# A hybrid decoder block on one Trainium2 core: the split left operands of the output projection placed at 16 different byte offsets

## The chip, the core and the metric

The kernel runs on one core of a Trainium2 chip. The core has TensorE (matmuls, "PE", and the loads of its stationary operand, "PEld"), VectorE ("DVE"), ScalarE ("ACT"), GpSimd ("POOL"), and SyncE ("SP"), which here only issues DMAs. SBUF is the on-chip memory of 128 partitions from which the engines read their operands; PSUM takes TensorE's results. The metric is the device time of one execution in microseconds (us), as the median of several runs.

## What is computed

One decoder block on a sequence of 2048 positions and 1024 channels, in float32. The reference, cut to the stages that matter here:

```python
h = rms_norm(x, g_norm[l]) * (1.0 + scale[:, None, :]) + shift[:, None, :]
proj = h @ w_in[l]
...
y_rnn = (hr * jax.nn.silu(z_rnn.astype(jnp.float32))).astype(dt) @ w_out_rnn[l]
...
y_attn = (o * jax.nn.silu(z_attn.astype(jnp.float32))).astype(dt) @ w_out_attn[l]
merged = jax.nn.sigmoid(g_r + bg_r) * y_rnn + jax.nn.sigmoid(g_a + bg_a) * y_attn
x = x + gate[:, None, :] * (merged @ w_o[l])
return rms_norm(x, g_final)
```

The change lies in the last product, `merged @ w_o`, which the kernel calls the output projection.

## The kernel before

Each product of two float32 matrices is made of three matmuls in the type `float32r`: both operands are split into a high part (a rounded copy, written by ScalarE in `hi_act`, L157) and a low part (what the copy leaves out, written by VectorE in `lo_dve`, L166, or by GpSimd in `lo_pool`, L163). `mm3` (L151) then adds high x high, high x low and low x high into one PSUM tile. `mm` (L149) is the only place that issues matmuls, so all of them carry that line; the profile tells them apart by their tiles. In `mm` the operand called `l` (lhsT) is the stationary one that is loaded by a weight load, and `r` is the moving one that streams past it.

The program has four stages. First the normalised input and the input projection (PSUM tiles X, Z, W, V, Y; operands S, T and b12), with the recurrence of the RG-LRU branch (tiles xr, xc, pg, gh and gl) between its products. Then the attention (sc, pT, o, with operands kq, pp, vh and wh), with the branch output projections (pj) filled in between. `steps` (L1652) is the generator of these fillers: eight jobs, two branches by four column blocks of 512 positions, each of eight row tiles m and eight steps k; each step issues one `mm3`. What the two branches give is multiplied by its gates, added, and stored to `meT` in HBM. Last, the output projection.

The output projection is `output(n)` (L1833), called for n = 0 to 3. Each call yields four row blocks r of 128 positions, 16 in all, and after each row block eight steps of `steps` are drawn, as long as there are any (L1864 to 1867). For each row block:

- xo, 128 x 1024, is loaded from x, and mraw, 128 x 8 x 128, from `meT` (L1837 and L1840).
- mh, the high part of mraw, is written by ScalarE, and ml, the low part, by VectorE (L1843 and L1844). Both tiles have 4096 bytes in a partition and three buffers each, which the row blocks use in turn.
- For each half q of the 1024 output columns a PSUM tile pq (four buffers) gets 8 x 3 = 24 matmuls. The stationary operand is a 128 x 128 piece of mh or ml, the moving one 512 columns of oh or ol, the split of w_o times the gate, which `output_operands` (L1825) makes once. A row block so has 48 weight loads and 48 matmuls.
- VectorE adds pq to xo (L1851), ScalarE squares and sums (L1854), small steps make the factor of the norm (L170 to L179), VectorE applies it (L1856), and SP stores ob (L1857).

The order of the attention stage is written out by hand; that of this last stage is made by a scheduler when the program is built, from the order in which the code issues the instructions. Each engine runs its own instructions in the program's order and waits on semaphores for the others. SBUF addresses are given by pools. The pool `fp` holds, in this order, oh, ol, gf, gate_b, xo, mraw, mh, ml, ob and ss, and the pool `wr` behind it holds pieces of the branch weights. Both lie in memory that the attention's pool `ap` has left.

Of the kernel before, what the change touches and what calls it, by code (L numbers as in the profile page):

```python
# [11 lines left out]
F32R = mybir.dt.float32r  # L12
# [8 lines left out]
P = 128  # L21
S = 2048
D = 1024
KT = D // P
# [65 lines left out]
def decoder_block(ctx, tc, x, c, positions, g_norm, w_mod, b_mod, w_in, b_gate, conv_w, conv_b,  # L90
# [4 lines left out]
    def T(pool, shape, dt, tag, **kw):  # L95
        cnt[0] += 1
        return pool.tile(shape, dt, tag=tag, name=f"{tag}_{cnt[0]}", **kw)
# [53 lines left out]
    def mm3(o, lh, ll, rh, rl, first=True, last=True, **kw):  # L151
        mm(o, lh, rh, first, False, **kw)
        mm(o, lh, rl, False, False, **kw)
        mm(o, ll, rh, False, last, **kw)

    def hi_act(o, i):
        nc.scalar.activation(o, i, AF.Copy)  # L157
# [7 lines left out]
    def lo_dve(o, i, h):  # L165
        return nc.vector.tensor_tensor(o, i, h.bitcast(F32), ALU.subtract).ins  # L166
# [14 lines left out]
    def rstd(ss):  # L181
        rstd_first(ss)
        rstd_last(ss)
# [921 lines left out]
    for t in range(6):  # L1105
        pieces = []
        i0 = t * P
        while i0 < (t + 1) * P:
            hd, i = divmod(i0, 96)
            n = min(96 - i, (t + 1) * P - i0)  # L1110
# [154 lines left out]
    for f in range(2):  # L1265
# [20 lines left out]
        n = 0  # L1286
# [528 lines left out]
    fp = pools.open("fp", bufs=1)  # L1815
# [17 lines left out]
    def output(n):  # L1833

        for r in range(4):
            xo = T(fp, [P, D], F32, "xo", bufs=2)
            nc.sync.dma_start(xo[:], xv[n, r])  # L1837
            t = T(fp, [P, KT, P], F32, "mraw", bufs=2)
            c0 = n * CH + r * P
            nc.sync.dma_start(t[:], meT[:, c0 : c0 + P].rearrange("(k p) j -> p k j", p=P))  # L1840
            th = T(fp, [P, KT, P], F32R, "mh", bufs=3)
            tl = T(fp, [P, KT, P], F32R, "ml", bufs=3)
            hi_act(th[:], t[:])  # L1843
            lo_dve(tl[:], t[:], th[:])  # L1844
            for q in range(2):
                cq = slice(q * CH, (q + 1) * CH)
                ps = T(pq, [P, CH], F32, "pq")
                for k in range(KT):
                    mm3(ps[:], th[:, k, :], tl[:, k, :], oh[:, k, cq], ol[:, k, cq],
                        first=k == 0, last=k == KT - 1)  # L1850
                nc.vector.tensor_tensor(xo[:, cq], ps[:], xo[:, cq], ALU.add)  # L1851
            ob = T(fp, [P, D], F32, "ob", bufs=1)
            ss = T(fp, [P, 3, 1], F32, "ss", bufs=4)
            nc.scalar.activation(ob[:], xo[:], AF.Square, accum_out=ss[:, 0])  # L1854
            rstd(ss)
            nc.vector.scalar_tensor_tensor(ob[:], xo[:], ss[:, 1], gf[:], ALU.mult, ALU.mult)  # L1856
            nc.sync.dma_start(outv[n, r], ob[:])  # L1857
            yield
# [5 lines left out]
    for n in range(NB):  # L1864
        for _ in output(n):
            for _ in range(KT):
                next(fill, None)
# [30 lines left out]
```

## Time and profile before

| what | value |
|---|---|
| median of 3 runs | 2237.18 us (2236.78 to 2237.21) |
| the profiled execution, its own time | 2235.07 us |
| span of its instructions | 2233.3 us |
| TensorE clock granted, mean | 0.994 |
| first and last matmul of the output projection start at | 1981.5 and 2224.6 us |
| weight loads and matmuls of the output projection | 768 each |

How to read the profile: it shows one execution. Busy times are in us, the mean of one instruction in nanoseconds (ns). A group such as `pq<-oh,mh` names the tile that is written and the tiles that are read. Matmuls are pipelined: the length shown for one of them (389 ns for 512 columns) overlaps the next one's, so their pace is read from the distance of their starts. The chain of waits is followed back from the last instruction: at each step to what released it, or to the instruction before it on its engine. In a list of stretches or of the timeline "x" is the number of instructions; "idle before" an instruction is time in which its engine had nothing to do.

### The profile page before, as it was taken

Reading aid. Unit: us, or ns where it says so; the run is one execution under the profiler, and the core shown is the slowest. Engines: PE = TensorE matmul, PEld = TensorE weight load, DVE = VectorE, ACT = ScalarE, POOL = GpSimd, SP = SyncE. Lnnn points to the kernel's source line nnn. Section 1 sums busy time; section 2 is a strip of 40 time slices with the busy share of each in tenths; the row PEclk is TensorE's granted clock in tenths of the full one; section 3 lists DMA queues with packets and bytes.
Section 4 is the critical chain, followed back from the end, with each engine's and each line's share of the span. In section 5 each row is a group of like instructions: output and inputs, shape, how many; then the busy total and the mean of one; then the engine's idle time right before and its main releaser. Section 6 shows DMA issues by size and latency. Waiting matters only on the chain.

```text
span 2233.3 us, 33998 instructions
## 1 busy us (share of the span) xinstructions
PE 2185.9 (98%) x11422; PEld 1851.1 (83%) x11422; DVE 1348.6 (60%) x2380; ACT 1256.2 (56%) x2481; POOL 978.3 (44%) x734
## 2 busy tenths in 40 slices
PE   8999999999999999999999999999999998999998
PEld 5998888888778998888888887888888887878886
DVE  5838887878455815544545442566677777666443
ACT  6638678668543627556556202667778887533211
POOL 2457777767557422222222102455566665332100
PEclk9999999999999999999999999999999999999999
DMA  8367887887998378888888988988988887899542
GB/s 286 117 211 259 287 295 269 292 282 269 326 282 288 114 229 271 286 286 280 287 288 278 343 291 286 285 265 259 271 255 264 246 262 216 254 338 284 155 132 85
DMA packets 428626, 573.64 MB, mean 257 GB/s; under 512 B 72134, under 2 KB 292514, under 8 KB 427428
## 3 DMA queue, kind: packets, MB, share of 16 engines
q1 hardware_dynamic: 390612, 451.73, 64.9%
q10 hardware_dynamic: 37648, 119.70, 14.0%
q8 instruction: 90, 1.47, 0.3%
q14 instruction: 84, 0.69, 0.1%
q0 software_dynamic: 192, 0.05, 0.0%
HBM read 357.44 MB, written 213.91 MB: 256 GB/s over the span
## 4 chain that ended last, share of the span: by engine, by line
PE 55%; DMA 6%; DVE 3%; ACT 3%; issue 2%; POOL 2%; SPq 1%; ACTq 0%; POOLq 0%; DVEq 0%
PE pj L149 11%; PE X L149 8%; PE V L149 7%; PE pq L149 7%; PE sc L149 4%; PE W L149 4%; PE Z L149 4%; PE o L149 4%; PE Y L149 3%; PE pT L1501 1%; DMA R<-in_w_in_dram 1%; PE pg L149 1%; PE pT L1514 1%; POOL S L163 1%; DMA gaT<-ev 1%
## 5 line engine op out<-in xcount | busy, mean ns | idle before, releaser
L149 PE MATMUL pj<-yh,S 128*128 128x512 f32 x1024 | 367.8, 403 | 9.7 <-ACT yh L157 4.8
L163 POOL TENSOR_TENSOR S<-R,S 128x512 fp32r<-128x512 f32 x168 | 252.2, 1509 | 175.0 <-ACT S L157 64.9
L149 PE MATMUL V<-T,S 128*128 128x512 f32 x1344 | 324.6, 390 | 3.7 <-DVE t L450 3.5
L149 PE MATMUL X<-T,S 128*128 128x512 f32 x1344 | 324.5, 390 | 2.9 <-POOL S L163 1.9
L149 PEld LDWEIGHTS V<-T,S 128*128 128x128 f32 x1344 | 251.8, 188 | 58.4 <-DVE t L450 2.4
L149 PEld LDWEIGHTS X<-T,S 128*128 128x128 f32 x1344 | 251.4, 188 | 58.0 <-POOL S L163 2.8
L149 PEld LDWEIGHTS pj<-yh,S 128*128 128x128 f32 x1024 | 193.2, 189 | 47.8 <-ACT yh L157 6.7
L149 PE MATMUL pj<-yl,S 128*128 128x512 f32 x512 | 201.6, 394 | 6.2 <-POOL yl L163 5.1
L1417 ACT ACTIVATE pp<-pp,st 128x256 f32<-128x256 f32 (+3 forms) x256 | 133.8, 524 | 94.0 <-DVE st L1416 92.9
L163 POOL TENSOR_TENSOR S<-s,S 128x512 fp32r<-128x512 f32 x84 | 128.9, 1535 | 113.5 <-ACT S L157 68.8
L149 PE MATMUL Z<-T,S 128*128 128x512 f32 x672 | 162.0, 390 | 0.0
L149 PE MATMUL Y<-T,S 128*128 128x512 f32 x672 | 161.8, 390 | 0.0
L149 PE MATMUL W<-T,S 128*128 128x512 f32 x672 | 161.6, 389 | 0.0
L149 PEld LDWEIGHTS W<-T,S 128*128 128x128 f32 x672 | 126.0, 188 | 26.9 <-issue 0.9
L149 PEld LDWEIGHTS Y<-T,S 128*128 128x128 f32 x672 | 125.9, 188 | 26.0
L149 PEld LDWEIGHTS Z<-T,S 128*128 128x128 f32 x672 | 125.9, 188 | 26.1
L166 DVE TENSOR_TENSOR ptl<-pT,pth 128x384 fp32r<-128x384 f32 (+1 forms) x160 | 97.9, 629 | 75.6 <-ACT pth L157 73.4
L163 POOL TENSOR_TENSOR s<-R,s 128x512 fp32r<-128x512 f32 x32 | 45.9, 1434 | 198.4 <-ACT s L157 172.1
L157 ACT ACTIVATE S<-R 128x512 fp32r<-128x512 f32 x168 | 101.7, 621 | 48.1 <-DMA R<-in_w_in_dram 21.1
L908 DVE SCALAR_TENSOR_TENSOR xc<-xr,par,xc 128x512 f32<-128x512 f32 x96 | 98.5, 1026 | 45.7 <-ACT xc L902 43.5
L1481 ACT ACTIVATE pp<-pp,M 128x256 f32<-128x256 f32 (+3 forms) x256 | 118.0, 523 | 9.9 <-DVE M L1604 9.9
L1416 DVE CUSTOM_DVE_ANT_0 pp<-sc,msk 128x256 f32<-128x256 f32 (+3 forms) x256 | 104.6, 449 | 23.6 <-PE sc L149 21.3
(334 smaller groups left out, 4731.3 us busy)
## 6 DMA issues: line engine op xcount, KB each, us to landing
sD<-S ACTq DMA_DIRECT2D x196, 512.0 KB, 4.1
S<-sD SPq DMA_DIRECT2D x196, 512.0 KB, 5.0
S<-wD SPq DMA_DIRECT2D x100, 512.0 KB, 5.4
R<-in_w_in_dram SPq DMA_DIRECT2D x136, 256.0 KB, 4.3
wD<-s ACTq DMA_DIRECT2D x64, 256.0 KB, 5.0
T<-in_w_mod_dram SPq DMA_DIRECT2D x8, 1024.0 KB, 12.0
vN<-ev SPq DMA_DIRECT2D x64, 128.0 KB, 2.7
zaT<-ev SPq DMA_DIRECT2D x32, 256.0 KB, 4.4
```

The lines of the kernel that those rows point to most:

```text
L149: nc.tensor.matmul(o, lhsT=l, rhs=r, start=st, stop=sp, **kw)
L157: nc.scalar.activation(o, i, AF.Copy)
L163: nc.gpsimd.tensor_tensor(o, i, h.bitcast(F32), ALU.subtract)
L166: return nc.vector.tensor_tensor(o, i, h.bitcast(F32), ALU.subtract).ins
L908: nc.vector.scalar_tensor_tensor(xc, xr[:, i : i + CH], cw(i), xc, ALU.mult, ALU.add)
L1416: nc.vector.tensor_tensor_reduce(pdst, s_ps, mask, 1.0, 3e38, ALU.add, ALU.min, m_)
L1417: nc.scalar.activation(pdst, pdst, AF.Exp, bias=m_, scale=-1.0, accum_out=l_)
L1481: nc.scalar.activation(pp, pp, AF.Copy, scale=w)
L1501: nc.tensor.transpose(pt[:, c0 + j * P : c0 + (j + 1) * P], pp[i][:, k * P : (k + 1) * P], ident)
L1514: nc.tensor.transpose(pt[:, c * P : (c + 1) * P], pp[:, half * P : (half + 1) * P], ident)
```

## The change

The tiles mh and ml get 128 elements more in each partition (4608 bytes in place of 4096), and in row block 4n + r the split starts at element o0 = 4 (4n + r), that is 16 (4n + r) bytes into the tile: 0 in the first row block, 240 in the last. The piece from there on, 8 x 128 elements without gaps, is used in place of the whole tile. What is written into it and read from it stays the same.

```diff
             c0 = n * CH + r * P
             nc.sync.dma_start(t[:], meT[:, c0 : c0 + P].rearrange("(k p) j -> p k j", p=P))
-            th = T(fp, [P, KT, P], F32R, "mh", bufs=3)
-            tl = T(fp, [P, KT, P], F32R, "ml", bufs=3)
-            hi_act(th[:], t[:])
-            lo_dve(tl[:], t[:], th[:])
+            o0 = 4 * (4 * n + r)
+            th, tl = (T(fp, [P, (KT + 1) * P], F32R, tag, bufs=3)[:, o0 : o0 + KT * P].rearrange("p (k j) -> p k j", k=KT)
+                      for tag in ("mh", "ml"))
+            hi_act(th, t[:])
+            lo_dve(tl, t[:], th)
             for q in range(2):
                 cq = slice(q * CH, (q + 1) * CH)
                 ps = T(pq, [P, CH], F32, "pq")
```

The matmuls below (`mm3(ps[:], th[:, k, :], tl[:, k, :], ...)`) are unchanged in the text and read from the new place.

## The prediction

> **What bounds the kernel now.** I read the page's first part, then the chain of waits over the last 275 us, then the groups of the tiles that the change touches.
>
> ```profile
> span 2233.3 us, 33998 instructions
> PE 2185.9 (98%) x11422; PEld 1851.1 (83%) x11422; DVE 1348.6 (60%) x2380; ACT 1256.2 (56%) x2481; POOL 978.3 (44%) x734
> ```
>
> TensorE is busy in 98% of the span, so what counts is the time between two matmuls, and what TensorE waits for. In the stage of the change the chain (start, length, what) says:
>
> ```profile
> 1970.96 7.01 DMA xo<-in_w_o_dram
> ...
> 1984.33 1.21 DVE ml L166
> ...
> 1994.44 6.80 DMA xo<-in_w_o_dram
> ...
> 2022.80 6.00 DMA R<-oT
> ...
> 2029.51 0.50 PE pj L149
> ...
> 2132.52 5.44 PE pj L149 x24
> 2137.96 87.05 PE pq L149 x384
> 2225.01 0.02 issue
> 2225.03 0.70 DVE xo L1851
> ...
> 2228.38 1.28 DVE ob L1856
> ```
>
> From 2029.51 to 2225.01 us the chain is TensorE alone, without a gap: output projection (pq) and the last branch projection (pj) in turn, then pq alone. The 384 matmuls at the end take 87.05 / 384 = 226.7 ns each. Before 2029.51 the chain runs through loads and small VectorE and ScalarE steps; after 2225.01 comes the tail of the last row block, which neither mh nor ml enters.
>
> **The change, part by part.** No instruction is added, removed or reordered: on every engine the built programs hold the same instructions in the same order. Four things differ.
>
> *1. The start of the left operand.* In both programs the buffers of mh and ml start 128 bytes past a multiple of 256. Row block 4n+r now starts 16(4n+r) bytes further on. Each of the 16 blocks has 48 weight loads and 48 matmuls; block 0 keeps its start, so 15 x 48 = 720 pairs change. The rows of their tiles (minimum, median, maximum in ns, then first and last start):
>
> ```profile
> L149 PEld LDWEIGHTS pq<-oh,mh x256: 186/188/189, 1981.3 to 2223.9; 128*128 128x128 f32 x128
> L149 PE MATMUL pq<-oh,mh x256: 389/389/494, 1981.5 to 2224.2; 128*128 128x512 f32 x128
> L149 PEld LDWEIGHTS pq<-oh,ml x256: 186/188/188, 1983.9 to 2224.4; 128*128 128x128 f32 x128
> ```
>
> A load takes 188 ns and has 226.7 until the next matmul: 39 ns of cover. The trace of before already has loads from other starts: the right operand b12 of the input projection lies 32 bytes past a multiple of 256 in the first pass (93 to 134 us) and exactly on one in the second, and the recurrence gate's gh lies 192 past one:
>
> ```profile
> L149 PEld LDWEIGHTS X<-S,b12h x112: 187/188/193, 96.2 to 801.0; 128*128 128x128 f32 x112
> L149 PEld LDWEIGHTS pg<-xh,gh x64: 187/187/188, 166.5 to 1220.0; 128*128 128x128 f32 x64
> ```
>
> 187 to 188 ns at the median, whatever the start. The distance from one pair to the next does depend on it a little. In the timeline (start, length, what) of the first pass, weights at +32, and of the second, weights at +0, the moving tile at +128 in both:
>
> ```profile
> 93.48 0.40 PE L149 MATMUL W<-S,b12h 128*128 128x256 f32 x2
> ...
> 96.36 0.40 PE L149 MATMUL X<-S,b12h 128*128 128x256 f32 x2
> ```
>
> ```profile
> 761.35 0.39 PE L149 MATMUL X<-S,b12h 128*128 128x256 f32 x2
> ...
> 764.20 0.40 PE L149 MATMUL V<-S,b12h 128*128 128x256 f32 x2
> ```
>
> Between the two rows of each lie 24 matmuls (eight groups of two on b12h and one on b12l): (96.36 - 93.48) / 24 = 120.0 ns and (764.20 - 761.35) / 24 = 118.8 ns for 256 columns. With 226.7 ns for 512 columns, 256 columns cost 106.7, so a pair costs its columns plus 13.3 ns at +128 and +32, plus 12.1 at +0. And loads of 188 ns follow each other every 120 ns, so a load holds its port for at most 120. The third place, with 512 columns and both operands at +192 between runs at +128:
>
> ```profile
> 164.92 1.97 PE L149 MATMUL W<-T,S 128*128 128x512 f32 x8
> 166.73 0.39 PE L149 MATMUL pg<-xh,gh 128*128 128x512 f32 x1
> ...
> 168.12 2.23 PE L149 MATMUL V<-T,S 128*128 128x512 f32 x9
> ```
>
> Six pg pairs take 168.12 - 166.73 = 1.39 us, 231.7 ns each, 30 ns too long in all; the nine V after them stand (2.23 - 0.39) / 8 = 230.0 ns apart, 26 ns too long, while the W before stood at (1.97 - 0.39) / 7 = 225.7. So a change of start disturbs some six to eight pairs by about 28 ns in all (an estimate from this one place). From 2034.60 on there are 6 blocks between pj runs, each with a change in and out, and 8 blocks at the end with one each: 20 x 28 ns = 0.6 us.
>
> Within a block of 48 the start stays the same, and there I take no change, as at +32. The bounds of that: -1.2 ns a pair (as at +0) or +5.0 (if a block stayed disturbed as pg is), over 720 pairs -0.9 to +3.6 us. But the eight starts that are odd multiples of 16 (384 pairs) have no row at all. For them, and so for the range, wider bounds: the fixed 13.3 ns vanish, as if they were a collision of the two reads, or they double, which is also what a port time of 120 ns doubled to 240 against 226.7 would add: +-13.3 x 720 = +-9.6 us. I take 0 for them too, since the nearest rows, 32 bytes apart, differ by little more than 1 ns.
>
> *2. ScalarE writes mh and VectorE writes ml at the new start.* One tile of before is written off such a boundary: xr, whose 512 elements start 12 bytes into a buffer, by both engines, beside aligned tiles of the same instruction and shape:
>
> ```profile
> L448 ACT ACTIVATE xr<-X x16: 577/590/599, 154.1 to 1185.7; 128x512 f32<-128x512 f32 x16
> L383 ACT ACTIVATE u<-X x56: 577/582/602, 142.5 to 1349.2; 128x512 f32<-128x512 f32 x56
> L450 DVE TENSOR_TENSOR xr<-V,u x16: 1087/1106/1134, 161.5 to 1193.8; 128x512 f32<-128x512 f32 x16
> L450 DVE TENSOR_TENSOR ev<-V,u x56: 676/692/692, 171.1 to 1251.7; 128x512 f32<-128x512 f32 x56
> ```
>
> ScalarE does not mind (590 against 582 ns). VectorE does: 1106 against 692, or 414 / 512 = 0.81 ns an element. So a write's start can matter on this chip. Whether a start that is a multiple of 16 but not of 32 or 64 pays is not in the trace; the bounds for an ml are 0 and 0.81 x 1024 = 0.83 us on top of the 1.2 us below, for at most 15 of them. [...]
>
> What hides it: after 2029.51 the buffers are three deep. VectorE's work on the stage and who waits:
>
> ```profile
> L157 ACT ACTIVATE mh<-mraw x16: 1042/1062/1067, 1980.2 to 2192.2; 128x1024 fp32r<-128x1024 f32 x16
> L166 DVE TENSOR_TENSOR ml<-mraw,mh x16: 1211/1225/1227, 1982.6 to 2193.3; 128x1024 fp32r<-128x1024 f32 x16
>   PE pq L149: 109.8, 12
> 2137.96:2225.01 87.05, 87.04 (x384) 71.75 (x383) 33.09 (x71) 14.22 (x26) 0.00 (x0) 1.00 0.36 118
> ```
>
> The splits of 12 blocks sat idle for 109.8 us until TensorE had freed the buffer, and each is used a block or more later, at 48 x 0.2267 = 10.9 us a block; VectorE is busy for 33.09 of the last 87.05 us (third figure). A split that is 0.83 us longer disappears there, and so do the additions (L1851) queued behind it, as four PSUM buffers stand before TensorE. Without that cover it would be 15 x 0.83 = 12.4 us. Before 2029.51 only two changed splits run, at 1984.33 (on the chain above) and here:
>
> ```profile
> 1994.20 1.21 DVE L166 TENSOR_TENSOR ml<-mraw,mh 128x1024 fp32r<-128x1024 f32 x1
> ```
>
> Behind them on VectorE stand the sums of fg, whose stores and loads SP issues, and the products xo (L1829). At most both delays reach the matmul of 2029.51: 2 x 0.83 = 1.7 us. Since every aligned row is flat and the one slow row splits 16 bytes, I take 0 and keep +1.7.
>
> *3. One wait moves.* Because the buffers are 512 bytes longer, the second mh (ScalarE, at about 1981 us) now also waits for the last store of an attention tile that lay in that memory, and for an instruction of its own engine before it.
>
> ```profile
> L1622 SPq DMA_DIRECT2D oT<-zt x32: 319/404/1206, 1455.1 to 1954.0; - x32
> DMA to landing us min/median/max: 4.3/6.1/7.8
> ```
>
> That store was issued no later than 1954.0 and landed no later than 1954.0 + 7.8 = 1961.8, some 19 us before it is asked for: 0. The older load of that queue for which the next weight split waited is covered by this wait and drops out there: 0.
>
> *4. Addresses behind the buffers* (wr, ob, ss) move by 3072 bytes, 12 x 256, with the same place within 256: 0.
>
> Sum: 0.6 + 0 + 0 + 0 = 0.6 us. The profiled execution took 2235.07 us (1.8 more than its span) and would take 2235.7; the three timed runs have a median of 2237.18, 0.09% higher, and on that scale the forecast is 2237.8 us.
>
> **The rivals.** About 0.2% (4.5 us) is the least that a measurement of this kernel tells from no change; spread over 720 pairs it is 6.2 ns each, and from there a price decides.
>
> *Weight loads from an odd multiple of 16 are slower (slower).* The fixed part of a pair doubles where the start is no multiple of 32: 384 x 13.3 = 5.1 us, 2242.3; or at every new start, 9.6 us, 2246.8. For it: half of the starts have no precedent, pg's pairs at +192 show that a start can cost 5 ns, and xr that it can cost far more on another engine. Against it: no row reaches 6.2 ns, and a load 39 ns longer would still be hidden. A load read twice over, 376 ns against 226.7, would be 720 x 149 = 107 us; nothing comes near that.
>
> *VectorE's write of ml pays (no change that can be seen).* ml at 2.05 us, the end up to 1.7 us later: 2237.8 + 1.7 = 2239.5. For it xr, against it that xr's start is no multiple of 16.
>
> *A collision is removed (faster).* Both reads of a pair start at +128 now; set apart, the fixed 13.3 ns go: 2237.2 - 9.6 = 2227.6. For it: b12 at +0 pays 1.2 ns less than at +128. Against it: at +32, set apart as well, it pays the same 13.3.
>
> *The change doesn't do what it says.* The offset could fall away in the allocation; in the built program the 16 starts differ, so this holds no chance of its own. Its time would be 2237.2.
>
> **How the numbers follow.** Forecast: 0.69. VectorE pays, hidden or up to 1.7 us: 0.07. Together within 0.2%: 0.76. The weight load slower by 5 to 10 us: 0.18, by far more: 0.01, so slower 0.19. Collision removed: 0.05, faster. The predicted time is 2237.8. The range goes up to 2246.8, the far bound of the slower load, and down to 2234.0: 0.9 us for pairs as at +0 and some 2 us because the profiled execution, too, was 2.1 us below the median. It leaves out the removed collision.
>
> **What would show it.** Right: loads of mh and ml at 188 ns in every block, mh at 1.06 us, blocks of 48 at 10.88 us but for some 30 ns each, and the last 384 matmuls in about 87.3 us. Wrong on the load: blocks longer than that by 0.3 us or more, every second one if 32 bytes is the unit, or all but the first. Wrong on VectorE: maxima of ml near 2.0 us, with the last gap before continuous matmuls later than 2029.51 by up to 1.7 us. Wrong on the collision: blocks of about 10.2 us. A missed forecast with blocks of 10.88 us would put the cause before 2029.51.

## The result

| | before | changed |
|---|---|---|
| median of 6 runs each | 2237.19 us | 2243.8 us |
| lowest and highest | 2233.96, 2242.9 | 2241.8, 2247.36 |
| span of the profiled execution | 2233.3 us | 2240.0 us |

The ratio is 1.0026, with a 95% interval from 1.0014 to 1.0038: slower by some 5.8 us, between 3.1 and 8.5. The forecast was 2237.8 us, with a range up to 2246.8.

The chain of waits of the changed kernel (start, length, what), from where TensorE runs without a gap:

```profile
2037.48 5.45 PE pj L149 x24
2042.93 11.20 PE pq L149 x48
...
2137.38 5.49 PE pj L149 x24
2142.87 88.89 PE pq L149 x384
2231.76 0.02 issue
2231.78 0.70 DVE xo L1852
...
2235.13 1.28 DVE ob L1857
```

Before, the same pieces were 5.44, 10.88, 5.44 and 87.05 us, and the stretch from the first pj row to the end of pq took 2225.01 - 2034.60 = 190.41 us. Now it takes 2231.76 - 2037.48 = 194.28: 3.87 us more. Of these the pq runs have 3.72 and the seven pj runs 0.16; nothing else in the chain of this stage got longer. The rest of the 6.7 us between the two profiled spans lies ahead of it: 2037.48 against 2034.60. There the first pq matmul starts 3.6 us later (1985.1 against 1981.5), and from it to 2037.48 the changed kernel is 0.7 us quicker. Up to the first mh the instructions are the same in the same order, and the kernels below, which have the same ones up to there, reach their first pq matmul anywhere from 1981.2 to 1990.2 us. So this part is within what differs from one execution to the next. The stage's 3.87 us lie within the interval of 3.1 to 8.5; that the change costs anything beyond them isn't shown.

The groups of the tiles (minimum, median, maximum in ns, first and last start) of the changed kernel:

```profile
L149 PEld LDWEIGHTS pq<-oh,mh x256: 186/188/192, 1984.9 to 2230.7; 128*128 128x128 f32 x128
L149 PE MATMUL pq<-oh,mh x256: 387/394/404, 1985.1 to 2230.9; 128*128 128x512 f32 x128
L157 ACT ACTIVATE mh<-mraw x16: 1041/1062/1066, 1983.5 to 2198.3; 128x1024 fp32r<-128x1024 f32 x16
L166 DVE TENSOR_TENSOR ml<-mraw,mh x16: 1211/1226/1226, 1985.8 to 2199.4; 128x1024 fp32r<-128x1024 f32 x16
```

The loads still take 188 ns at the median, mh 1062 and ml 1226: neither the load as the profile shows it nor the two splits got longer. The matmul did, 394 in place of 389 ns, and so did the distance from one matmul to the next. It isn't the clock: over the last 384 matmuls the granted clock, the third figure from the end, stands at 1.00, as it did before:

```profile
2142.87:2231.76 88.89, 88.87 (x384) 71.82 (x383) 33.08 (x71) 14.21 (x26) 0.00 (x0) 1.00 0.36 116
```

The mean distance in each row block, from the starts in the trace (distances over 260 ns, which hold a wait, left out; in the first two blocks short runs of pq and pj alternate):

| offset, bytes | 0 | 16 | 32 | 48 | 64 | 80 | 96 | 112 |
|---|---|---|---|---|---|---|---|---|
| ns a pair | 227.7 | 226.9 | 233.2 | 233.2 | 233.3 | 232.0 | 234.2 | 233.3 |

| offset, bytes | 128 | 144 | 160 | 176 | 192 | 208 | 224 | 240 |
|---|---|---|---|---|---|---|---|---|
| ns a pair | 232.4 | 233.3 | 233.3 | 229.9 | 229.0 | 233.2 | 233.3 | 227.1 |

Before, each of blocks 2 to 15 stood at 226.7. In this table the offsets 0, 16 and 240 cost next to nothing (240 is 16 before 256; its block of 227.1 starts with three longer distances and then stands at 226.7); all others cost 2 to 7.5 ns a pair on the average. They do so throughout the block and not only at its beginning, and in a fixed rhythm: at 64 the distances are 236 and 231 ns in turn, at 192 they go round in 232, 226 and 229.

### The profile page after: what moved, and what is told of

It is laid out like the page before. It is cut to its first block, busy times and chain, and to the rows that moved or that the text cites. A ratio compares the mean times of both kernels' runs of the same rounds, so it can differ in the third digit from the quotient of the medians.

```text
span 2240.0 us, 33999 instructions
## 1 busy us (share of the span) xinstructions
PE 2191.2 (98%) x11422; PEld 1852.4 (83%) x11422; DVE 1347.9 (60%) x2380; ACT 1255.6 (56%) x2481; POOL 979.5 (44%) x734
## 4 chain that ended last, share of the span: by engine, by line
PE 56%; DMA 7%; issue 2%; DVE 2%; ACT 2%; POOL 2%; SPq 1%; ACTq 0%; POOLq 0%; DVEq 0%
PE pj L149 11%; PE pq L149 8%; PE X L149 8%; PE V L149 7%; PE o L149 4%; PE sc L149 4%; PE W L149 4%; PE Z L149 4%; PE Y L149 3%; PE pT L1501 1%; DMA R<-in_w_in_dram 1%; PE pg L149 1%; PE pT L1514 1%; DMA vraw<-vN 1%; DMA S<-wD 1%
```

## The experiments

Two theories for the table. A: what counts is the distance between the start of the stationary operand and that of the moving one. B: what counts is where the stationary operand starts. A third, C, lays the cost on the change of the start from block to block. The kernels for which no interval is given ran once; they are read by the starts of their matmuls and not by their time.

**One offset for all blocks.**

```diff
-            o0 = 4 * (4 * n + r)
+            o0 = 16
```

> All 16 row blocks have the offset 64 in place of 0 to 240, so mh and ml start 192 bytes past a multiple of 256 throughout, oh and ol stay at 128. Theory A (what counts is the distance between the starts of the stationary and the moving operand) and theory B (what counts is where the stationary operand itself starts) expect the pace of the changed kernel's block at +64, 233.3 ns a pair, in every block: 384 x 233.3 = 89.6 us for the last 384 matmuls (87.05 before, 88.89 changed), and 768 x 6.6 = 5.1 us on the whole. Theory C (what costs is that the start changes from block to block) expects 226.7 ns within the blocks, 87.05 us.

Its chain, one block and the last eight:

```profile
2123.07 11.20 PE pq L149 x48
...
2139.74 89.61 PE pq L149 x384
```

89.61 / 384 = 233.4 ns: A and B as expected, and C falls. Over 11 runs the ratio to before is 1.0019 (1.0009 to 1.0030), 4.3 us with 2.0 to 6.7; the stage, measured as above, took 195.06 us, 4.65 more than before.

**Both operands moved alike, and the moving one alone.** oh and ol get 64 elements more and a start of 64 bytes; mh and ml have 64 in the first kernel and 0 in the second.

```diff
-    oh = T(fp, [P, KT, D], F32R, "oh")
-    ol = T(fp, [P, KT, D], F32R, "ol")
+    oh, ol = (T(fp, [P, KT * D + 64], F32R, tag)[:, 16 : 16 + KT * D].rearrange("p (k d) -> p k d", k=KT)
+              for tag in ("oh", "ol"))
...
-            o0 = 4 * (4 * n + r)
+            o0 = 16
```

> mh and ml at +64 as in the run before, and oh and ol moved by 64 bytes as well, so that both operands start 192 past a multiple of 256. Theory A expects 226.7 ns a pair and 87.05 us for the last 384 matmuls, no time lost. Theory B expects 233.3 ns and 89.6 us, 5.1 us on the whole.

> mh and ml at offset 0 (start at 128) in every block, oh and ol moved by 64 bytes to 192. Theory A expects the pace of the changed kernel's block whose stationary operand starts 64 before the moving one (offset 192): 229.0 ns, 87.9 us for the last 384 matmuls. Theory B expects 226.7 ns and 87.05 us.

The chain of the first kernel, both moved:

```profile
2133.51 5.45 PE pj L149 x24
2138.96 87.10 PE pq L149 x384
```

The chain of the second, only the moving operand:

```profile
2141.05 5.49 PE pj L149 x24
2146.54 87.93 PE pq L149 x384
```

87.10 us with both at +64, against 89.61 with one of them there: the same stationary place is dear or free depending on the moving operand. And the moving operand alone makes 87.93 us, 229.0 ns a pair, which is what the changed kernel showed at 192: in both the stationary operand starts 64 bytes before the moving one, in one at 128 and 192, in the other at 64 and 128. With the stationary one 64 bytes behind, it was 233.4. A holds, B falls. Over 11 runs the kernel with both moved stands at 0.9994 (0.9984 to 1.0005). What remains is paid at the change of place: a block between two pj runs took 10.92 us in place of 10.88, and its starts show these 42 ns in the first ten or so distances (224 to 236 ns), with 226.7 from there on.

**A distance of 256.** `o0 = 64` in all blocks.

> The changed kernel with one offset of 256 bytes in all row blocks: stationary and moving operand are 256 apart modulo 512 but both start at 128 modulo 256. If the distance counts modulo 256, 226.7 ns a pair and 87.05 us for the last 384 matmuls; if it counts in whole, as one more place at which the operands differ, some 233 ns and 89.5 us.

Its chain:

```profile
2135.23 5.44 PE pj L149 x24
2140.67 87.05 PE pq L149 x384
```

A distance of 256 is as good as 0 (226.7 ns a pair at both), so the distance counts modulo 256 (shown at 0 alone: for 256, and through the steps of 512 bytes between the pieces k for multiples of 512). This kernel also has the longer tiles and the moved addresses behind them, and its stretch from the first pj row (2037.31) to the end of pq took 190.41 us, exactly as before: the padding by itself costs the stage nothing.

**Steps of 4 bytes.** `o0 = 4 * n + r`, offsets 0 to 60.

> The changed kernel with steps of 4 bytes in place of 16: offsets 0 to 60. In the changed kernel the offset 16 cost nothing (227.1 ns) and 32 cost 233.2. Theories A and B expect 226.7 ns for the first blocks and some 233 from 32 on, with the turn somewhere between 16 and 32. VectorE's ml: if only starts off a multiple of 16 pay, as the tile xr at +12 bytes did, 12 of the 16 ml take about 1.23 + 0.83 = 2.05 us and those at 0, 16, 32 and 48 take 1.23; ScalarE's mh stays at 1.06.

The chain's blocks at 8, 12, 16, 20, 24 and 28, of which three are free and three are not:

```profile
2042.57 11.07 PE pq L149 x48
...
2059.12 10.88 PE pq L149 x48
...
2075.44 10.88 PE pq L149 x48
...
2091.77 11.19 PE pq L149 x48
...
2108.41 11.09 PE pq L149 x48
...
2124.94 10.88 PE pq L149 x48
```

There is no turning point, as I had expected one: 8 costs 230.7 ns, 12 and 16 are free (226.7), 20 costs 233.2, 24 costs 231.1, 28 is free (226.7), 32 costs 233.2 again. From 32 to 60 all cost, most of them 233, 44 and 60 some 230. Where a distance came twice (16, 32, 48, 64, 192), in different kernels and behind different blocks, its price was the same within 0.4 ns. So in these kernels the price with 512 columns belongs to the distance, but it isn't a function that one could guess between two measured points. The VectorE group of the same kernel:

```profile
L166 DVE TENSOR_TENSOR ml<-mraw,mh x16: 1212/1226/1229, 1984.0 to 2198.1; 128x1024 fp32r<-128x1024 f32 x16
```

No ml takes longer than 1229 ns at any start, 12 of 16 of them off a multiple of 16. The start of such a gapless write costs VectorE nothing here.

**Only the low part moved.** mh at offset 0, ml at 64.

```diff
-                      for tag in ("mh", "ml"))
+                      for tag, o0 in (("mh", 0), ("ml", 16)))
```

> Only ml is moved, by 64 bytes in all row blocks; mh stays at the place of oh and ol. One weight load in three (that of the low x high matmul) then starts elsewhere. If each load is paid by itself, a third of 6.6 ns: 226.7 + 2.2 = 228.9 ns a pair and 87.9 us for the last 384 matmuls. If one displaced load disturbs the pairs behind it, as a change of place disturbed six to eight pairs at +192 in the recurrence, no pair comes to rest: 230 to 233 ns, 88.3 to 89.5 us.

```profile
2131.34 11.09 PE pq L149 x48
...
2147.88 88.75 PE pq L149 x384
```

88.75 / 384 = 231.1 ns. One displaced load in three costs 4.4 ns a pair on the average, or 13.3 for each displaced load, twice the 6.6 that it costs when all are displaced. So a load isn't paid by itself: the second expectation holds. The starts show more than it said: from the third pair of a block on, the distances repeat in threes, 228 ns from high x high to high x low, 229 on to low x high and 236 from there to the next high x high. All three are above 226.7, and 9 of the 13 ns fall on the one behind the displaced load.

**256 columns.** In the prediction most of the rows for other starts had 256 columns. Here each run of 24 matmuls is made as two with half the columns, once at offset 0 and once with the 16 offsets.

```diff
-                for k in range(KT):
-                    mm3(ps[:], th[:, k, :], tl[:, k, :], oh[:, k, cq], ol[:, k, cq],
-                        first=k == 0, last=k == KT - 1)
+                for h in range(2):
+                    ch = slice(q * CH + h * 256, q * CH + h * 256 + 256)
+                    for k in range(KT):
+                        mm3(ps[:, h * 256 : h * 256 + 256], th[:, k, :], tl[:, k, :], oh[:, k, ch], ol[:, k, ch],
+                            first=k == 0, last=k == KT - 1)
```

> Offset 0, and each run of 24 matmuls of 512 columns in the output projection made as two runs of 24 with 256 columns, so 96 pairs a row block. It is the base of the next run: 120.0 ns a pair, as the pairs of 256 columns whose operands both start at 128 have in the input projection.

> The 16 offsets of the changed kernel with 256 columns a matmul. If the distance of the starts costs the same for each weight load, every block from +32 to +224 shows 120.0 + 6 = 126 ns a pair. If 256 columns behave as b12's pairs did (119.9 at 160 past the moving operand's start, 118.6 at 128 past it), no block is more than 1 ns above 120.0, and some lie below; then rows of 256 columns could not have told the price of 512.

The chain at offset 0:

```profile
2151.18 92.16 PE pq L149 x768
```

The chain with the 16 offsets:

```profile
2146.73 91.12 PE pq L149 x768
```

92.16 / 768 = 120.0 ns, and the 16 offsets are faster. By blocks, from the starts: 118.3 at 32 and at 48, 117.8 at 64, 118.6 at 80, 117.3 at 96, 120.0 at 112, 120.1 at 128, 119.8 at 144, 120.0 at 160, 118.1 at 176, 117.8 at 192, 116.7 at 208 and at 224, 120.0 at 240. The sign is turned round: with 256 columns a distance costs nothing or gains up to 3.3 ns, with 512 it costs up to 7.5. b12's 119.9 at 160 is met (120.0); its 118.8 at 128 is not (120.1), though both operands start at the same places modulo 256 there, so with 256 columns the distance isn't all that counts; what else does, no run shows. At 160 the same distance costs nothing with 256 columns and 6.6 ns with 512: rows of 256 columns could not tell the price of 512.

**The attention.** Its pj matmuls stand further apart than 226.7, and its own tiles lie elsewhere (pp at 0, vh to yw at 192). Two kernels without the change move these tiles:

```diff
-                self.st = T(ap_, [P, 2, 2, 4, 2], F32, "st", bufs=3)
+                self.st = T(ap_, [P, 2, 2, 4, 2], F32, "st", bufs=4)
...
-            self.M = M = T(ap_, [P, 2, 4, 2], F32, "M", bufs=2)
+            self.M = M = T(ap_, [P, 2, 4, 2], F32, "M", bufs=3)
```

> The kernel before, with two small attention tiles given one buffer more (st four, M three), which moves the attention's tiles behind them: pp starts 128 past a multiple of 256 instead of 0, and vh, wh, pth, ptl, zt, yw 128 instead of 192, as the branch projection's own operands always did. mh and ml are as before. During the attention the starts of neighbouring pj matmuls are 230.6 ns apart on average, against 226.7 in a run of their own. Theory A1 (that excess, too, comes from neighbours whose operands start elsewhere) expects about 227 ns there, and 849 x 4 = 3.4 us less, 5 us with the attention's own pairs. Theory A2 (the excess comes from the changes between matmuls of 128, 256 and 512 columns, wherever they start) expects 230.6 again and no change within 0.1%.

```diff
+            if not pads:
+                pads.append(T(ap_, [P, 8], F32, "pad1"))
             th = T(ap_, [P, CH], F32R, "pth", bufs=4)
             tl = T(ap_, [P, CH], F32R, "ptl", bufs=4)
+            if len(pads) < 2:
+                pads.append(T(ap_, [P, 56], F32, "pad2"))
```

> The kernel before, with pth and ptl, the moving operands of the attention's sums, moved by 32 bytes, so that vh and wh start 224 past them modulo 256; all else stays in its place within 256. In the run of half matmuls 256 columns took 116.7 ns at 224 against 120.0 at 0. If that carries over, the 672 pairs of 256 columns of the attention (118.4 ns apart by their starts before) come to about 116.7: 672 x 1.7 = 1.1 us less, 0.05% faster at most, which the times will hardly show and the starts will. If the changes between shapes decide there, as in the run with the attention's tiles at 128, 118.4 again.

Mean distances during the attention, from the starts (those up to 30 ns over the time of the columns alone):

| | pj before pj, 512 columns | attention's sums, 256 columns | time to before, 95% |
|---|---|---|---|
| before | 230.6 | 118.4 | |
| pp, vh, wh, pth, ptl at 128 | 230.5 | 118.7 | 1.0000 (0.9989 to 1.0011) |
| pth and ptl 32 bytes on | 229.7 | 117.0 | 0.9989 (0.9976 to 1.0002) |

In the kernels above whose attention is that of before, the two means are 230.6 to 230.7 and 118.3 to 118.4, so a difference of 0.3 ns counts. The first kernel falsifies what I had hoped for: with these tiles at 128, as pj's own operands are, pj doesn't recover (0.1 to 0.2 ns). It doesn't free the attention of differing starts altogether, for 168 matmuls of the scores still read kq at 0 against a stationary operand at 128. Whether the rest of the excess comes from them, or from the changes of shape, wasn't tried by itself. The second does what the curve of 256 columns says, 1.4 ns less a pair; that pj, too, came 0.9 ns nearer was not foreseen, and shows that a part of its excess does hang on its neighbours' starts. The median of its 12 runs, 2236.91 us, is the lower one (before: 2240.37 over 17 runs), but the interval of the ratio includes 1, so it is no version that is shown to beat the kernel before.

## Why the prediction was right and where it was wrong

Right: mh and ml took no longer (1062 and 1226 ns at the median, against 1062 and 1225), the loads stayed at 188 ns, the moved addresses cost nothing (190.41 us in the kernel with a distance of 256), the second mh had to wait for no store (0.20 us of idle time before it, until mh, its own engine's, was done), and the part of the effect that is shown lies in the distance of the pairs from 2034.60 on. The price per pair lies within its bounds.

That the median of 2243.8 us lies within the range is luck. The forecast was no change, 2237.8; the range reached up to 2246.8 by the rival of slower loads, with a doubled fixed part at every new start, and neither that reason nor its 13.3 ns a pair was met.

The step that failed is in part 1: "Within a block of 48 the start stays the same, and there I take no change, as at +32." The sum over blocks 1 to 15 is 15 x 48 x 5.14 = 3.7 us (mean excess of the table over 226.7; the passing disturbance at the entry of each block is in it), and the pj runs between (5.44 to 5.49 in place of 5.44 us) bring it to the 3.87 us of the stage. The value 0 came from b12's rows, which had half the columns, and the runs with 256 columns show that there the sign is another. And the rows were sorted by where the stationary operand starts, while the distance to the moving one is what counts.

The upper one of the two bounds next to that step, +5.0 ns a pair and 3.6 us, was the answer to within 0.3 us, but by luck as well. It came from the only row with 512 columns, pg, whose two operands both start at 192, so that their distance is 0; in that place a longer run goes back to 226.7 (87.10 us for 384). pg's six pairs, at 231.7 ns, were stretched as the first distances of a block, at a change of place, are in the kernel with both operands moved (228, 229, 234, 235, 225 and 230 ns), which agrees with what the prediction said of them.

The port time of 120 ns that stands beside the far bound of the range, +-13.3 ns a pair, was an estimate of mine, from loads of 188 ns that follow each other every 120; no run shows a port. In its place the runs showed 2 to 7.5 ns a pair for the distances that cost, with loads of 188 ns at the median before and with the 16 offsets.

The changes between blocks, put at 28 ns each, cost about 50 ns for a way in and out in the kernel with both operands moved (10.92 - 10.88, and 5.45 - 5.44): the right size.

In part 2 the reading of xr was wrong. I took its 1106 ns on VectorE, against 692, for the price of the 12 bytes. Steps of 4 bytes on ml show no such price (1212 to 1229 ns). Two groups of the same form in the profile need not read the same way: xr is written through

```python
total(xr[:, 3:].rearrange("p (j r) -> p j r", r=4), ps, u, nat)
```

where `nat` makes both inputs be read with a stride of 128 elements. That is the difference that the code leaves; it wasn't tried by itself. The 0 of part 2 took 16 bytes for the unit that xr's start splits: no run shows such a unit. In its place the runs showed an ml at 1211 to 1226 ns from the 16 starts of the changed kernel, and at 1212 to 1229 from those 4 bytes apart, 12 of which are off a multiple of 16.

Of the rivals, the slower load had the right sign and the wrong mechanism: odd multiples of 16 are not the dear ones (16 and 240 stand at 226.9 and 227.1 ns; 32, 64 and 128 at 233.2, 233.3 and 232.4). The removed collision is the nearest to what the runs show, for the relation of the two operands is what counts, but the place where both start alike, from which the change moved away, is one of the cheapest for 512 columns (226.7 ns). The chance of 0.76 for a change within 0.2% looks too high: the ratio's middle is 0.26%, though its interval begins at 0.14% and the stage's 3.87 us alone are 0.17%.

With nothing but the distance of the two starts changed, a pair took 226.7 ns at 0 or 233.4 at 64 (87.05 and 89.61 us for 384). What lies behind it, no run here shows.

## What to carry to other kernels

Where TensorE ran pair after pair in this kernel, the distance from the stationary operand's start to the moving operand's set up to 3% of the pace with 512 columns (226.7 ns a pair at 0 and at 256, up to 234.2 at 96; 3.87 us of 2237 for a change of one stage). So look at this distance; keep it the same for every load of a run (one displaced load in three cost 4.4 ns a pair), at 0 for 512 columns, and measure it anew for another column count: with 256 columns 0 was not the cheapest (120.0 ns, against 116.7 at 208 and 224). Padding that makes a tile longer shifts all tiles behind it, so look at where they come to lie. And compare the shape, and the way in which an operation walks through memory, before a row of the profile is carried over to another operation: here pairs of 256 columns (120.0 ns at 160, as at 0) did not tell those of 512 (233.3, against 226.7), nor xr's 1106 ns the 1212 to 1229 of ml.

## What the runs showed of the hardware

- The pace of float32r pairs with 512 columns depended on the distance of the two operands' starts in bytes: 226.7 to 227.1 ns at 0, 12, 16, 28 and 240, up to 234.2 at 96, and 226.7 again at 256. Where it was longer, the times from one matmul to the next repeated in a fixed rhythm (236 and 231 ns in turn at 64). With 256 columns it was 120.0 at 0 and 116.7 at 208 and 224.
- One displaced load in three cost 13.3 ns for each (231.1 ns a pair), two times the 6.6 that it cost where all were displaced.
- The length of the load in the profile, 188 ns at the median before and with the 16 offsets, didn't show any of this; the distance between matmul starts did.
- VectorE and ScalarE wrote gapless tiles of 1024 elements at the same speed from each of 16 starts, 0 to 60 bytes in steps of 4 (ml 1212 to 1229 ns, mh 1042 to 1070).
